# First norm's affine rows and the layer projection's rows asked for one at a time, at pairs 0, 1 and 3 of the output projection's second half

## The chip, the cores and the metric

The kernel runs on one core of a Trainium2 chip. The metric is the device time of one execution in microseconds. Before the change the median of three runs is 1655.25 us (1653.83 to 1656.07).

## The reference, cut to what matters

One decoder layer over 256 tokens of width 2048, all in float32. The change lies where step 2 below ends (the output projection and the first LayerNorm) and where step 4's second factor is prepared.

```
# 1. two token mixers (gated linear attention, forgetting attention) -> merged (256 x 2048)
x = layer_norm(ALPHA * x + merged @ w_out, ln1_g, ln1_b)          # 2.
g = causal_dwconv(x @ w_gate, conv_w, conv_b)                     # 3.
x = layer_norm(ALPHA * x + (gelu(g) * (x @ w_up)) @ w_down, ln2_g, ln2_b)
x = x + sigmoid(x @ w_ple_gate) * (p @ w_ple_proj)                # 4.

layer_norm(x, g, b) = (x - mean) * rsqrt(var + 1e-5) * g + b      # along the 2048 channels
```

The products keep float32 accuracy: each float32 operand is split into a high part (rounded to the matmul's format, "hi") and a rest ("lo"), and hi*hi, hi*lo and lo*hi are summed in PSUM.

## The kernel before, in words

**Weights.** The weights lie in memory as numbered units of 128 x 2048 floats (1 MB), and are used in the order of their numbers. A unit comes in two halves of 512 KB (`raw130_0`, `raw130_1`). For each half, `prep` (lines 191 to 230) issues a load on SP's queue into one of four "raw" buffers (line 205); then ScalarE (ACT) copies it to a "hi" buffer (line 212), and VectorE (DVE) subtracts hi from raw into a "lo" buffer (line 217); then TensorE (PE) multiplies. So the load of a half waits until DVE has made the lo of the half four places before it in the raw ring. `unit` (line 235) prepares up to two units ahead of the one that it hands out. There are six hi and six lo buffers.

**SP's queue** is kept in the order in which the Python code asks for the loads (line 118). The instructions of the other engines are put in order by the compiler's scheduler, which also follows priorities (`tc.high_priority`, `tc.keep_in_program_order`); each engine then works strictly in that order.

**The output projection** is `residual("wo", ...)` (line 1232; the function is at line 1053). It has two column halves, `nh` 0 and 1, of eight units each: 120 to 127, then 128 to 135. One unit covers a pair of 128-row blocks of the contraction, so the code counts "pairs" 0 to 7 in each half. A normal pair has 24 matmuls of 512 columns (line 334): two blocks, two token halves, three products, two banks. In the first half pairs 1, 2, 4 and 5 go another way with seven products (line 354). In the second half the last two pairs (units 134, 135) are held back as a tail (`tail=2`) and done token half by token half, so that the LayerNorm of the first 128 tokens (`t` = 0) can begin while the second 128 are still being multiplied.

**Loads between the pairs.** `mid` maps a pair to calls made after that pair: in the first half `mid1` loads the residual `z1` at pairs 2 and 3, and `mid1g` at pair 7 loads the norm's gain and bias, each a row of 2048 floats broadcast to 128 partitions (`lnb00` and `lnb01`, 1 MB of SBUF each, `load_gain`, line 1109). In the second half `mid1x` at pair 0 only reserves the four buffers of `x1T` (the norm's transposed output), and `ple_prep(0)` at pair 3 (line 1115) loads the layer projection's first half (`praw00`, `praw01`, 512 KB each, in raw buffers) and the transposed `p` (`pTr`, 256 KB), with the same hi and lo split on ACT and DVE. All of these but `praw` and `pTr` sit in a pool of 15 buffers of 8 KB per partition (`s8`).

**The first LayerNorm** (`ln_steps`, line 1001, run from `end1`, line 1149): the evacuation adds PSUM to `z1` (line 1066) and takes statistics (1067); DVE joins them (1009, 1010), GpSimd raises to the power -1/2 (1011), DVE makes the shift (1012). Column groups 1 and 3 are normalised on ACT (line 1025), and get gain and bias only after the transposition, as per-partition scalars (1043 on ACT, 1045 on DVE, taking turns within one group). Groups 0 and 2 get gain and bias from `lnb00` and `lnb01` on DVE (1020, 1022). The order of the groups is 1, 0, 3, 2. Each group is transposed on PE (line 1033) into one of two PSUM buffers, so the third transposition waits until the first group has been read, the fourth until the second has. Between them PE works on the layer projection (`pp`, line 334). Then the MLP's first units (136, 137, 138) begin on the first 128 tokens (line 303), and the normalised rows are later multiplied by gain and bias (line 1104) and written out for the next residual.

Of the kernel before, what the change touches and what calls it, by code (L numbers as in the profile page):

```python
# [19 lines left out]
P = 128  # L20
# [28 lines left out]
WOW = ((1, 2, 4, 5), ())  # L49
# [15 lines left out]
def tile_block(ctx: ExitStack, tc: tile.TileContext, wu, xw, wfv, wpp, xT_in, x_in, pT_in, wlr,  # L65
               chan, gnorm, lng, ident_in, mask_in, cmask_in, out):
    nc = tc.nc
# [15 lines left out]
    st1 = [cst.tile([P, 4, 6], F32, name=f"st1{t}") for t in range(2)]  # L83
# [3 lines left out]
    def s8(shape, dt=F32, name=None):  # L87
        t = big.tile([P, S8W], dt, tag="S8", name=name)
        n = int(np.prod(shape[1:]))
        t = t[:shape[0], :n]  # L90
        if len(shape) == 3:
            return t.rearrange("p (a b) -> p a b", b=shape[2])
        if len(shape) == 4:
            return t.rearrange("p (a b c) -> p a b c", b=shape[2], c=shape[3])
        return t
# [10 lines left out]
    def t2(name):  # L106
        return sm.tile([P, 512], F32, tag="t2", bufs=6, name=name)
# [7 lines left out]
    def copy(o, i, scale=1.0):  # L115
        nc.scalar.activation(o, i, AF.Copy, bias=0.0, scale=scale)
# [796 lines left out]
    mT = [s8([P, 4, 512], F32R, name=f"mT{i}") for i in range(4)]  # L913
# [139 lines left out]
    def residual(name, act, K, zs, stats, mid, done=None, end=None, ws=((), ())):  # L1053

        for nh in range(2):
            def zp(t, c, nh=nh):
                g = 2 * nh + c
                return zs[t][:, g * 512:g * 512 + 512]

            def ev(t, c, ps, nh=nh, zp=zp):  # L1060
                zc = zp(t, c)
                with tc.high_priority(P_STAT):
                    if ws[nh]:
                        nc.vector.tensor_tensor(zc, zc, ps, ALU.add)
                    else:
                        nc.vector.scalar_tensor_tensor(zc, zc, ALPHA, ps, ALU.mult, ALU.add)
                    nc.vector.bn_stats(stats[t][:, 2 * nh + c, :], zc)

            def joined(ms, zp=zp):
                p1, p5, p7, p6 = ms  # L1070
                u = t2("ju")

                def onto(t, c, p):
                    with tc.high_priority(P_STAT):
                        nc.vector.scalar_tensor_tensor(zp(t, c), zp(t, c), ALPHA, p, ALU.mult,
                                                       ALU.add)

                def plus(o, a, p):
                    with tc.high_priority(P_STAT):
                        nc.vector.tensor_tensor(o, a, p, ALU.add)  # L1080

                with tc.high_priority(P_STAT):
                    tc.keep_in_program_order(nc.scalar.activation(u, p1, AF.Copy, bias=0.0,
                                                                  scale=1.0))
                    tc.keep_in_program_order(nc.vector.scalar_tensor_tensor(
                        zp(0, 0), zp(0, 0), ALPHA, p1, ALU.mult, ALU.add))
                plus(u, u, p6)
                onto(0, 1, u)
                plus(u, u, p7)
                onto(1, 0, u)  # L1090
                plus(u, u, p5)
                onto(1, 1, u)
                plus(zp(0, 1), zp(0, 1), p5)

            x_half(f"{name}{nh}", act, K, ev, tail=2 if nh == 1 else 0, mid=mid[nh],
                   done=done if nh == 1 else None, end=end if nh == 1 else None, ws=ws[nh],
                   joined=joined, lean=name == "dn")

    def affine(zs, gb_, after, gs=range(4)):
        for t in range(2):  # L1100
            for g in gs:
                zc = zs[t][:, g * 512:g * 512 + 512]
                for b, op in zip(gb_, (ALU.mult, ALU.add)):
                    tc.keep_in_program_order(nc.vector.tensor_tensor(
                        zc, zc, b[:, g * 512:g * 512 + 512], op))
                    yield
            after(t)

    def load_gain(li):
        gb_ = [s8([P, 2048], name=f"lnb{li}{i}") for i in range(2)]  # L1110
        for i in range(2):
            nc.sync.dma_start(gb_[i], lng[2 * li + i].broadcast_to([P, 2048]))
        return gb_

    def ple_prep(half):

        w = [s8([P, 2048], F32R, name=f"pw{half}{i}") for i in range(2)]
        pt_ = s8([P, 2, 512], F32R, name=f"pTs{half}")
        pTs = [pt_[:, k, :] for k in range(2)]
        for k in range(2):  # L1120
            raw = ring.tile([P, 1024], F32, tag="raw", bufs=4, name=f"praw{half}{k}")
            nc.sync.dma_start(raw, wpp[half, :, k * 1024:k * 1024 + 1024])
            o = slice(k * 1024, k * 1024 + 1024)
            copy(w[0][:, o], raw)
            nc.vector.tensor_tensor(w[1][:, o], raw, w[0][:, o].bitcast(F32), ALU.subtract)
        pT = t2("pTr").rearrange("p (k t) -> p k t", t=S)
        nc.sync.dma_start(pT, pT_in)
        for k in range(2):
            copy(pTs[k][:, 0:256], pT[:, k, :])
            nc.vector.tensor_tensor(pTs[k][:, 256:512], pT[:, k, :],  # L1130
                                    pTs[k][:, 0:256].bitcast(F32), ALU.subtract)
        return w, pTs

    z1 = [s8([P, 2048], name=f"z1{t}") for t in range(2)]
    gain = [None, None]

    def mid1(t):
        nc.sync.dma_start(z1[t], x_in[t])

    def mid1g():  # L1140
        gain[0] = load_gain(0)

    x1T = []
    pq, first = [], []

    def mid1x():
        x1T.extend(s8([P, 4, 512], F32R, name=f"x1T{g}") for g in range(4))
# [81 lines left out]
                    turn1(G[3])  # L1229
            first.extend(ps)  # L1230

    residual("wo", mT, 16, z1, st1, ({2: lambda: mid1(0), 3: lambda: mid1(1), 7: mid1g}, {0: mid1x, 3: lambda: pq.append(ple_prep(0))}), end=end1, ws=WOW)
    mixers.append(affine(z1, gain[0], lambda t: nc.gpsimd.dma_start(x1d[t], z1[t]),
                         [g for g in range(4) if g not in AFF_DVE]))

# [92 lines left out]
    def mid2a():  # L1328
        gain[1] = load_gain(1)
# [5 lines left out]
    pb, pq = [], []  # L1335
# [224 lines left out]
```

## Time and profile before

| | |
|---|---|
| median of three runs | 1655.25 us |
| the profiled execution's own time | 1654.46 us |
| its span, first to last instruction | 1652.7 us |
| PE busy in the span | 1645.3 us |
| DVE, ACT busy | 1235.4, 882.4 us |
| moved by DMA | 394.23 MB, 239 GB/s in the mean |
| granted PE clock | 1.0 |

In the rows of the profile, times are in microseconds from the span's start. A timeline row reads: start, length, engine, line, operation, what it writes and reads, the count of merged instructions, and in brackets how long the engine sat idle before it and what ended that. PE's matmuls are pipelined: their lengths overlap, and one follows another by less than its length. SPq rows are DMA issues; where ACT waits for a load, its row begins just after the load has landed.

### The profile page before, as it was taken

How to read it: one execution, taken by the hardware profiler on the slowest of the kernel's cores; microseconds unless marked ns; L12 is line 12 of the kernel's file. 1: busy time of each engine (PE TensorE's matmuls, PEld its weight loads, DVE VectorE, ACT ScalarE, POOL GpSimd, SP SyncE). 2: the span in 40 equal slices, each digit the busy share in tenths (PEclk: the TensorE clock that was granted, in tenths of full speed). 3: DMA queues.
4: the chain of work that ended last, by engine and by line, in shares of the span. 5: the costliest groups of instructions: out<-in, count | busy, mean ns of one | idle time of the engine just before them, and what ended most of it. 6: DMA issues, size and time to landing. Idle time of an engine off the chain costs nothing.

```text
span 1652.7 us, 24308 instructions
## 1 busy us (share of the span) xinstructions
PE 1645.3 (100%) x8956; PEld 1427.4 (86%) x8956; DVE 1235.4 (75%) x1819; ACT 882.4 (53%) x1268; POOL 94.7 (6%) x217
## 2 busy tenths in 40 slices
PE   9999999999999999999999999999999999999998
PEld 8988888888888888888888888888888888888887
DVE  6656658768756767787688788888887687888884
ACT  6745445545555555555465545554455565466643
POOL 0000000000000100000010011111110011010000
PEclk9999999999999999999999999999999999999999
DMA  7665555555553875567747678888886588799354
GB/s 298 234 203 178 165 188 181 180 180 176 182 180 128 322 278 199 194 207 292 270 169 235 229 253 325 330 319 333 327 288 228 196 296 304 285 335 355 144 188 169
DMA packets 107527, 394.23 MB, mean 239 GB/s; under 512 B 12504, under 2 KB 13408, under 8 KB 104464
## 3 DMA queue, kind: packets, MB, share of 16 engines
q1 hardware_dynamic: 97296, 354.72, 61.9%
q0 software_dynamic: 9968, 37.76, 6.0%
q8 instruction: 70, 1.15, 0.3%
q14 instruction: 49, 0.40, 0.1%
q10 hardware_dynamic: 144, 0.20, 0.0%
HBM read 365.36 MB, written 27.27 MB: 238 GB/s over the span
## 4 chain that ended last, share of the span: by engine, by line
PE 94%; DMA 3%; DVE 2%; ACT 1%; issue 0%; SPq 0%; POOL 0%; ACTq 0%; DVEq 0%
PE psu L290 9%; PE psg L290 9%; PE psm L290 7%; PE dn L334 7%; PE gr L334 5%; PE gv L334 5%; PE pg L334 5%; PE psu L292 5%; PE psg L292 5%; PE psm L292 4%; PE psa L290 4%; PE fv L496 3%; DMA raw<-in_wu_dram 2%; PE dn L354 2%; PE dn0m L354 2%; PE psfq L290 2%
## 5 line engine op out<-in xcount | busy, mean ns | idle before, releaser
L217 DVE TENSOR_TENSOR lo<-raw,hi 128x1024 fp32r<-128x1024 f32 x502 | 611.4, 1224 | 257.8 <-ACT hi L212 255.8
L212 ACT ACTIVATE hi<-raw 128x1024 fp32r<-128x1024 f32 x502 | 528.9, 1059 | 464.8 <-DMA raw<-in_wu_dram 127.5
L290 PE MATMUL psu<-x1T,hi 128*128 128x512 f32 x688 | 236.0, 389 | 0.0
L290 PE MATMUL psg<-x1T,hi 128*128 128x512 f32 x672 | 230.5, 389 | 0.0
L292 PE MATMUL psu<-x1T,lo 128*128 128x256 f32 x688 | 189.9, 276 | 0.0
L292 PE MATMUL psg<-x1T,lo 128*128 128x256 f32 x672 | 185.5, 276 | 0.0
L290 PE MATMUL psm<-xT,hi 128*128 128x512 f32 x512 | 175.8, 391 | 0.0
L290 PEld LDWEIGHTS psu<-x1T,hi 128*128 128x128 f32 x688 | 129.2, 188 | 26.6
L290 PEld LDWEIGHTS psg<-x1T,hi 128*128 128x128 f32 x672 | 126.1, 188 | 26.1
L292 PE MATMUL psm<-xT,lo 128*128 128x256 f32 x512 | 141.4, 276 | 0.0
L292 PEld LDWEIGHTS psu<-x1T,lo 128*128 128x128 f32 x688 | 129.2, 188 | 0.0
L292 PEld LDWEIGHTS psg<-x1T,lo 128*128 128x128 f32 x672 | 126.1, 188 | 0.0
L290 PEld LDWEIGHTS psm<-xT,hi 128*128 128x128 f32 x512 | 96.1, 188 | 19.8
L334 PE MATMUL dn<-hi,hT 128*128 128x512 f32 x352 | 97.8, 389 | 0.0
L292 PEld LDWEIGHTS psm<-xT,lo 128*128 128x128 f32 x512 | 96.2, 188 | 0.2
L290 PE MATMUL psa<-oT,hi 128*128 128x512 f32 x256 | 87.8, 389 | 0.0
L334 PEld LDWEIGHTS dn<-hi,hT 128*128 128x128 f32 x352 | 66.0, 188 | 13.7
L334 PE MATMUL gv<-hi,xT 128*128 128x512 f32 x256 | 72.3, 394 | 0.0
L334 PE MATMUL gr<-hi,xT 128*128 128x512 f32 x256 | 72.1, 394 | 0.0
L292 PE MATMUL psa<-oT,lo 128*128 128x256 f32 x256 | 70.7, 276 | 0.0
L334 PE MATMUL pg<-hi,x2T 128*128 128x512 f32 (+1 forms) x224 | 60.0, 376 | 0.0
L290 PEld LDWEIGHTS psa<-oT,hi 128*128 128x128 f32 x256 | 48.1, 188 | 10.0
(356 smaller groups left out, 3075.6 us busy)
## 6 DMA issues: line engine op xcount, KB each, us to landing
raw<-in_wu_dram SPq DMA_DIRECT2D x528, 512.0 KB, 4.8
comb<-in_wu_dram SPq DMA_DIRECT2D x22, 768.0 KB, 8.7
tsd<-comb POOLq DMA_DIRECT2D x22, 512.0 KB, 7.2
top<-tsd SPq DMA_DIRECT2D x22, 512.0 KB, 6.1
fvraw<-in_wfv_dram SPq DMA_DIRECT2D x15, 524.0 KB, 7.9
rawf<-in_wu_dram SPq DMA_DIRECT2D x14, 512.0 KB, 9.4
top<-in_wu_dram SPq DMA_DIRECT2D x22, 256.0 KB, 7.0
hi<-hsd POOLq DMA_DIRECT2D x22, 256.0 KB, 5.2
```

Of the source, the lines that this page charges most:

```text
L212: c = nc.scalar.activation(hi, raw, AF.Copy, bias=0.0, scale=1.0)
L217: return nc.vector.tensor_tensor(lo, raw, hi.bitcast(F32), ALU.subtract)
L290: nc.tensor.matmul(ps, lhsT=hi[i // 8 if hoff == 0 else 0][:, w0 % 1024:w0 % 1024 + P], rhs=a[:, kt % 4, :], start=first and i == 0, stop= ...
L292: nc.tensor.matmul(ps[:, 256:512], lhsT=lo[i // 8 if hoff == 0 else 0][:, w0 % 1024:w0 % 1024 + P], rhs=a[:, kt % 4, 0:256], start=False, ...
L334: nc.tensor.matmul(bs[j][:, 0:m], lhsT=x, rhs=v[:, o:o + m], start=first and i == 0, stop=last and i == 2)
L354: nc.tensor.matmul(ps, lhsT=a, rhs=v, start=m and first and i == 0, stop=m and last and i == 2)
L496: nc.tensor.matmul(fbk[t][c][:, 0:n], lhsT=x, rhs=w[:, o:o + n], start=kt == 0 and i == 0, stop=kt == 15 and i == 2)
```

## The change

The output projection's second half gets other calls between its pairs. `ple_prep(0)` moves from pair 3 to pair 0; the gain row is asked for at pair 1 and the bias row at pair 3, instead of both at pair 7 of the first half; `x1T`'s buffers are reserved at pair 3 instead of 0. `load_gain`, which the second norm uses too, issues the same two loads as before.

```
-    def load_gain(li):
-        gb_ = [s8([P, 2048], name=f"lnb{li}{i}") for i in range(2)]
-        for i in range(2):
-            nc.sync.dma_start(gb_[i], lng[2 * li + i].broadcast_to([P, 2048]))
+    def load_row(li, i):
+        row = s8([P, 2048], name=f"lnb{li}{i}")
+        nc.sync.dma_start(row, lng[2 * li + i].broadcast_to([P, 2048]))
+        return row
+    def load_gain(li):
+        gb_ = []
+        for i in range(2):
+            gb_.append(load_row(li, i))
         return gb_
...
-    def mid1g():
-        gain[0] = load_gain(0)
+    gain1 = gain[0] = []
+    def mid1g(i):
+        gain1.append(load_row(0, i))
...
-    residual("wo", mT, 16, z1, st1, ({2: lambda: mid1(0), 3: lambda: mid1(1), 7: mid1g}, {0: mid1x, 3: lambda: pq.append(ple_prep(0))}), end=end1, ws=WOW)
+    residual("wo", mT, 16, z1, st1, ({2: lambda: mid1(0), 3: lambda: mid1(1)}, {0: lambda: pq.append(ple_prep(0)), 1: lambda: mid1g(0), 3: lambda: (mid1x(), mid1g(1))}), end=end1, ws=WOW)
```

**SP, the loads from unit 131 on.** SP's queue before, from the bias row to the layer projection's loads:

```order
L1112 DMA lnb01_7570<-in_lng_dram 128x2048
L205 DMA raw130_0_7585<-in_wu_dram 128x1024
L205 DMA raw130_1_7591<-in_wu_dram 128x1024
L205 DMA raw131_0_7625<-in_wu_dram 128x1024
L205 DMA raw131_1_7631<-in_wu_dram 128x1024
L205 DMA raw132_0_7661<-in_wu_dram 128x1024
L205 DMA raw132_1_7667<-in_wu_dram 128x1024
L205 DMA raw133_0_7697<-in_wu_dram 128x1024
L205 DMA raw133_1_7703<-in_wu_dram 128x1024
L1122 DMA praw00_7736<-in_wpp_dram 128x1024
L1122 DMA praw01_7740<-in_wpp_dram 128x1024
L1127 DMA pTr_7744<-in_pT_dram 128x512
```

And now, from the place behind unit 130 to unit 134:

```order
L1127 DMA praw00_7620<-in_wpp_dram 128x1024
L1127 DMA praw01_7624<-in_wpp_dram 128x1024
L1132 DMA pTr_7628<-in_pT_dram 128x512
L205 DMA raw131_0_7634<-in_wu_dram 128x1024
L205 DMA raw131_1_7640<-in_wu_dram 128x1024
L1111 DMA lnb00_7670<-in_lng_dram 128x2048
L205 DMA raw132_0_7672<-in_wu_dram 128x1024
L205 DMA raw132_1_7678<-in_wu_dram 128x1024
L205 DMA raw133_0_7708<-in_wu_dram 128x1024
L205 DMA raw133_1_7714<-in_wu_dram 128x1024
L1111 DMA lnb01_7748<-in_lng_dram 128x2048
L205 DMA raw134_0_7750<-in_wu_dram 128x1024
```

The layer projection's two halves take the raw buffers in which unit 131 lay before, and every half from 131 to 133 comes two places later in the ring; from 134 on the places are the old ones. The two 1 MB rows have moved from ahead of 130 to ahead of 132 and of 134. On ACT and DVE the projection's splits have moved with their loads, from between 133 and 134 to between 130 and 131.

**DVE in the first LayerNorm.** DVE before, from the first group's bias (line 1022) to the shift of the second token half (line 1012 of `mv_7879`); `z10` is the first token half, `z11` the second, `lny_7920` the affine step of group 1:

```order
L1022 SCALAR_TENSOR_TENSOR z10_7247<-z10_7247,mv_7878,lnb01_7570 128x512
L1066 SCALAR_TENSOR_TENSOR z11_7248<-z11_7248,wo1_10_7583 128x512
L1020 SCALAR_TENSOR_TENSOR z10_7247<-z10_7247,mv_7878,lnb00_7569 128x512
L1067 BN_STATS st11_85<-z11_7248 128x6
L1022 SCALAR_TENSOR_TENSOR z10_7247<-z10_7247,mv_7878,lnb01_7570 128x512
L1066 SCALAR_TENSOR_TENSOR z11_7248<-z11_7248,wo1_11_7584 128x512
L1045 TENSOR_SCALAR lny_7920<-ptl101_7915,chn_81 128x128
L1067 BN_STATS st11_85<-z11_7248 128x6
L1009 BN_AGGR mv_7879<-st11_85 128x2
L1010 TENSOR_SCALAR mv_7879<-mv_7879 128x1
L1045 TENSOR_SCALAR lny_7920<-ptl101_7915,chn_81 128x128
L1012 TENSOR_SCALAR mv_7879<-mv_7879 128x1
```

And now the same twelve:

```order
L1066 SCALAR_TENSOR_TENSOR z11_7248<-z11_7248,wo1_10_7579 128x512
L1022 SCALAR_TENSOR_TENSOR z10_7247<-z10_7247,mv_7878,lnb01_7748 128x512
L1067 BN_STATS st11_85<-z11_7248 128x6
L1020 SCALAR_TENSOR_TENSOR z10_7247<-z10_7247,mv_7878,lnb00_7670 128x512
L1066 SCALAR_TENSOR_TENSOR z11_7248<-z11_7248,wo1_11_7580 128x512
L1022 SCALAR_TENSOR_TENSOR z10_7247<-z10_7247,mv_7878,lnb01_7748 128x512
L1067 BN_STATS st11_85<-z11_7248 128x6
L1045 TENSOR_SCALAR lny_7920<-ptl101_7915,chn_81 128x128
L1009 BN_AGGR mv_7879<-st11_85 128x2
L1010 TENSOR_SCALAR mv_7879<-mv_7879 128x1
L1012 TENSOR_SCALAR mv_7879<-mv_7879 128x1
L1045 TENSOR_SCALAR lny_7920<-ptl101_7915,chn_81 128x128
```

The evacuations of the second token half stand one place earlier, and the second of group 1's affine steps now stands behind line 1012, which waits for GpSimd, instead of ahead of it.

**ACT in the same place.** ACT before, with the weight copies of units 137 and 138 and the affine steps of group 1:

```order
L212 ACTIVATE hi137_1_7841<-raw137_1_7839 128x1024
L1043 ACTIVATE lny_7920<-ptl101_7915,chn_81 128x128
L212 ACTIVATE hi138_0_8003<-raw138_0_8001 128x1024
L1043 ACTIVATE lny_7920<-ptl101_7915,chn_81 128x128
L212 ACTIVATE hi138_1_8008<-raw138_1_8006 128x1024
L116 ACTIVATE x1T1_7622<-lny_7920 128x4x128
```

And now:

```order
L212 ACTIVATE hi137_1_7841<-raw137_1_7839 128x1024
L1043 ACTIVATE lny_7920<-ptl101_7915,chn_81 128x128
L212 ACTIVATE hi138_0_8003<-raw138_0_8001 128x1024
L212 ACTIVATE hi138_1_8008<-raw138_1_8006 128x1024
L1043 ACTIVATE lny_7920<-ptl101_7915,chn_81 128x128
L116 ACTIVATE x1T1_7745<-lny_7920 128x4x128
```

The second affine step of group 1 now stands behind both copies of unit 138. A further exchange, of the same two kinds of DVE instruction, lies just ahead: the first evacuation (line 1066 on `wo1_00`) now stands before `lo136_1` instead of behind it.

## The prediction

> **What bounds the kernel now.** I read the page first, then the table of windows, PE's waits and timeline, and last the timelines of SP, ACT and DVE from 780 to 845 us, where all that moves lies. The page says that the chain that ended last is PE:
>
> ```profile
> span 1652.7 us, 24308 instructions
> PE 94%; DMA 3%; DVE 2%; ACT 1%; issue 0%; SPq 0%; POOL 0%; ACTq 0%; DVEq 0%
> ```
>
> So moving loads pays only if PE waits for something that they hold up. The table of windows (PE's busy time stands first, DMA share and GB/s last) shows the second half of the output projection and the LayerNorm behind it:
>
> ```profile
> core 0: us, PE busy (x) PEld busy (x) DVE busy (x) ACT busy (x) POOL busy (x), PEclk, DMA share, GB/s
> 797.00:812.00 15.00, 15.00 (x67) 12.11 (x66) 10.35 (x9) 5.82 (x6) 0.00 (x0) 1.00 0.70 234
> 836.00:845.00 9.00, 7.89 (x43) 6.12 (x42) 6.91 (x16) 7.67 (x13) 0.55 (x1) 1.00 0.00 0
> ```
>
> PE is full while the projection runs and loses 1.11 us in the norm. PE's timeline shows where, and when it needs units 131 and 132 (each lo is used behind two matmuls on hi):
>
> ```profile
> 780.56 1.07 PE L334 MATMUL wo<-hi,mT 128*128 128x512 f32 x4
> ...
> 808.49 0.62 PE L334 MATMUL wo<-lo,mT 128*128 128x512 f32 x2
> ...
> 813.93 0.62 PE L334 MATMUL wo<-lo,mT 128*128 128x512 f32 x2
> ...
> 826.17 0.61 PE L334 MATMUL wo<-hi,mT 128*128 128x512 f32 x2
> 826.81 0.50 PE L334 MATMUL wo<-lo,mT 128*128 128x512 f32 x1
> ...
> 840.57 0.66 PE L1033 MATMUL ptl<-ident,z 128*128 128x128 f32 x4 [0.93 <-DVE lny L1045]
> ...
> 842.80 0.66 PE L1033 MATMUL ptl<-ident,z 128*128 128x128 f32 x4 [0.18 <-DVE x1T L855]
> ```
>
> Two matmuls take 0.62 us where one takes 0.39, so one follows another by 0.23. Counting 24 to a unit on from 780.56, where unit 126 begins behind the last pair of the seven-product kind, the row at 808.49 is the first lo of unit 131 and that at 813.93 of 132. The row at 826.81 is the first use of `lo135_1`; it should have come at 826.17 + 0.45 = 826.62, so PE lost 0.19 there. The third transposition waited 0.93 us for DVE, the fourth 0.18.
>
> **The feed of units 131 to 134.** The issues on SP, then the copies to hi on ACT, which begin about 0.1 us after a load has landed:
>
> ```profile
> 781.85 1.00 SPq L1112 DMA_DIRECT2D lnb<-in_lng_dram  x2
> 797.86 0.33 SPq L205 DMA_DIRECT2D raw<-in_wu_dram  x1
> 799.00 0.33 SPq L205 DMA_DIRECT2D raw<-in_wu_dram  x1
> 800.13 0.33 SPq L205 DMA_DIRECT2D raw<-in_wu_dram  x1
> 804.20 0.33 SPq L205 DMA_DIRECT2D raw<-in_wu_dram  x1
> 812.05 0.33 SPq L205 DMA_DIRECT2D raw<-in_wu_dram  x1
> ```
>
> ```profile
> 788.03 1.06 ACT L212 ACTIVATE hi<-raw 128x1024 fp32r<-128x1024 f32 x1 [0.19 <-DMA raw<-in_wu_dram]
> 794.18 1.06 ACT L212 ACTIVATE hi<-raw 128x1024 fp32r<-128x1024 f32 x1 [5.08 <-DMA raw<-in_wu_dram]
> 795.41 1.06 ACT L212 ACTIVATE hi<-raw 128x1024 fp32r<-128x1024 f32 x1 [0.18 <-DMA raw<-in_wu_dram]
> 801.86 1.06 ACT L212 ACTIVATE hi<-raw 128x1024 fp32r<-128x1024 f32 x1 [5.38 <-DMA raw<-in_wu_dram]
> 804.68 1.06 ACT L212 ACTIVATE hi<-raw 128x1024 fp32r<-128x1024 f32 x1 [1.76 <-DMA raw<-in_wu_dram]
> 807.17 1.06 ACT L212 ACTIVATE hi<-raw 128x1024 fp32r<-128x1024 f32 x1 [1.43 <-DMA raw<-in_wu_dram]
> 818.84 1.06 ACT L212 ACTIVATE hi<-raw 128x1024 fp32r<-128x1024 f32 x1 [0.94 <-DMA raw<-in_wu_dram]
> ```
>
> And DVE, where the lo are made:
>
> ```profile
> 796.63 4.61 DVE L217 TENSOR_TENSOR lo<-raw,hi 128x1024 fp32r<-128x1024 f32 x4
> 819.93 2.48 DVE L217 TENSOR_TENSOR lo<-raw,hi 128x1024 fp32r<-128x1024 f32 x2 [0.71 <-ACT hi L212]
> 827.95 2.46 DVE L217 TENSOR_TENSOR lo<-raw,hi 128x1024 fp32r<-128x1024 f32 x2 [1.19 <-ACT hi L212]
> 831.64 0.67 DVE L1066 SCALAR_TENSOR_TENSOR z<-z,wo 128x512 f32<-128x512 f32 x1
> ```
>
> The four lo from 796.63 are those of 129 and 130: DVE makes them late, behind the first half's evacuation, and in the same order after the change. Each frees a raw buffer, and SP's issues at 797.86, 799.00 and 800.13 follow them. Before, the first three were `raw131_0`, `raw131_1` and `raw132_0`; they had landed when ACT began at 801.86, 804.68 and 807.17. Now the first two are `praw00` and `praw01`, `pTr` follows at once, and `raw131_0` is third.
>
> What is removed is little: the two 1 MB rows went out at 781.85 and delayed unit 130 (5.08 us of idle ACT ahead of 794.18), but its lo waited for DVE until after 796.63 anyway. So that delay cost nothing, and its removal brings nothing.
>
> What is added. When does `raw131_0` land? The upper bound is the same place in the old burst, 807.1, plus `pTr` in front of it. A full queue delivers 512 KB in 1.23 us (795.41 - 794.18; between 788.03 and 794.18 come two rows and half a unit, five times 512 KB, in 6.15), so `pTr`, half of that, makes it 807.7. The lower bound is the lone load's 801.76 (3.9 us after its issue) and from there that full rate: 1.23 + 0.62 + 1.23 more, 804.8. I take 807.0, nearer to the burst with the same issue times. Then hi is done at 807.1 + 1.06 = 808.2, lo at 809.4. PE wants it at 808.49: a new wait of 0.9 us.
>
> From there, at 1.23 us per 512 KB: `raw131_1` 808.2, `lnb00` 810.7, `raw132_0` (issued at 804.20 at the earliest, behind the row) 811.9; its lo is done at 814.3. PE wants it at 813.93 + 0.9: no second wait, with half a microsecond left. `raw134_0` takes that buffer now, so it is issued at 814.3 instead of 812.05, and has `raw132_1`, 133 and the bias row ahead of it: 813.1, 814.4, 815.6, 818.1, so it lands at 819.3 and its lo begins at 820.5. Before it began at 819.93: **0.6 us later**. `raw136_0` takes its place in the ring, so the pair of lo that began at 827.95 begins 0.6 later too.
>
> Which of these two delays reaches the end? DVE ran from 827.95 without a break to the second evacuation at 831.64. By the count, PE had finished that bank at 826.81 + 14 x 0.23 + 0.39 = 830.4, so DVE was 1.2 us behind PE there, and DVE sets the time of the norm. A delay of PE by 0.9 less the 0.19 that no longer arises stays inside that, and inside the 0.93 that PE idles later. **So the new wait is paid out of idle time that was there; the 0.6 us on DVE is not.** The exchange of the first evacuation with `lo136_1` leaves the sum of DVE's work up to the statistics the same: 0.
>
> **The order inside the LayerNorm.** DVE and ACT before:
>
> ```profile
> 838.70 0.41 DVE L1045 TENSOR_SCALAR lny<-ptl,chn 128x128 f32<-128x128 f32 x1
> ...
> 840.11 0.40 DVE L1045 TENSOR_SCALAR lny<-ptl,chn 128x128 f32<-128x128 f32 x1
> 840.86 0.21 DVE L1012 TENSOR_SCALAR mv<-mv 128x1 f32<-128x1 f32 x1 [0.35 <-POOL mv L1011]
> ...
> 842.07 0.68 DVE L855 TENSOR_TENSOR x1T<-ptl,x1T 128x512 fp32r<-128x512 f32 x1
> ```
>
> ```profile
> 838.57 1.05 ACT L212 ACTIVATE hi<-raw 128x1024 fp32r<-128x1024 f32 x1
> 839.52 0.44 ACT L1043 ACTIVATE lny<-ptl,chn 128x128 f32<-128x128 f32 x1
> ```
>
> The third transposition waited for the second affine step of DVE, done at 840.51. That step now stands behind line 1012, which waits for GpSimd until 840.86; an instruction follows it by some 0.13, so the step runs from 840.99 to 841.39. On ACT the affine step ahead of it now stands behind another copy of 0.95 (839.52 - 838.57): 840.47 to 840.91, which agrees. So the third transposition comes 0.88 later, at 841.45. From there PE has 842.80 - 840.57 - 0.18 = 2.05 of work to the fourth: 843.5 instead of 842.8, and the operand that it waited 0.18 for (842.07 + 0.68, likewise some 0.6 later) is there. **0.7 us**, with 0 (if the work before it shortens as much) and 0.9 as bounds. Queued behind line 1012 on DVE is all of `x1T`, so the units of the MLP begin that much later; nothing behind shows idle PE that could give it back. Elsewhere the change permutes buffers of the pool one for one, with equal lifetimes: 0. The gain row lands at 810.7, the bias row at 818.1, and both are first read after 833: 0.
>
> Sum: 0.6 + 0.7 = +1.3 us. Against the profiled execution (1654.46, of which the span is 1652.7) this gives 1655.8; against the median of 1655.25, 0.8 above that execution, 1656.5.
>
> **A page against the trace.** A lone 512 KB took 801.76 - 797.86 = 3.9 us here. The Trainium skill, "DMA: Bandwidth & Descriptors", section "Anatomy of one DMA", puts a DMA at 2.0 us plus its bytes at 436 GB/s (fitted for GpSimd's path), as an estimate 3.2 us for these 512 KB, and a burst at 1.2 us for each. By it `raw131_0` would land near 804 and PE would not wait at all; the row at 807.17 (9.3 us after the burst began, for three such loads) says otherwise, and the trace decides.
>
> **The rivals.** (a) *The queue runs full at once.* At 1.23 us per 512 KB behind 801.76, `raw131_0` lands at 804.8, `raw132_0` at 809.7, its lo is done at 812.1, `raw134_0` is issued as before and lands 5.0 us later at 817.1, and DVE's chain comes 1.6 earlier, as far as PE allows. With the 0.7 of the norm's order: -0.9; with that at nothing, no more than the 1.11 + 0.19 that PE idles: -1.3. For it speaks the rate behind 788.03, against it the burst behind 797.86. 1654.0 to 1655.2. It is also what the page above would make of the burst. (b) *The queue stays slow, and the kernel is slower.* The window from 797 to 812 ran at 234 GB/s, 2.24 us per 512 KB. At that pace `raw131_0` lands at 807.4, `raw132_0`, behind the 1 MB row, at 816.3, its lo is done at 818.7, 4.4 later than in the sum, and `raw134_0` with it: 0.6 + 4.4 + 0.7 = +5.7, 1661.0. It decides from the point where `lo132_0` comes after 816.3, 2 us later than I have it. Against it: up to five transfers are then in flight, as behind 788.03, not three. (c) *It does nothing*, since all is hidden: 1655.2. For it: PE idle and DVE behind PE, so both terms are small; against it: the new order on DVE is certain.
>
> **How the numbers follow.** The forecast, with its neighbours from 0 to +3.3, gets 0.58, (a) and (c) together 0.24, (b) 0.14, and 0.04 stays for what I don't see. The bound for "same" is 0.2%, 3.3 us, about what a measurement of this kernel can tell from no change. Faster than that needs more than the idle that there is: the 0.04. Slower is (b), from +3.3 on: 0.14. Same: 0.58 + 0.24 = 0.82. The range goes from -1.4 (a) to +3.9, between the forecast and (b), and leaves out most of (b) and the unseen: 1653.8 to 1659.2.
>
> **What would show it.** Right: PE's first lo of unit 131 waits 0.5 to 1.7 us for DVE or DMA, the wait of 0.19 at 135 is gone, the third transposition waits longer than 0.93 for line 1045, and the MLP begins 1 to 2 us later. Wrong: no wait at 131 (then (a)); a wait at 132 of microseconds (then (b)); the norm's waits as before; or a shift that arises elsewhere, after 870 or before 797.

## The result and the profile after

| | before | after |
|---|---|---|
| median of 22 runs each, taken side by side | 1654.86 us | 1657.58 us |
| ratio, 95% interval | | 1.0019 (1.0013 to 1.0025) |
| span of the profiled execution | 1652.7 us | 1655.4 us |

The change makes the kernel 0.19% slower: by the ratio +3.1 us (2.2 to 4.1), where +1.3 was forecast. It lies inside the range, but is over twice the forecast.

PE's waits after, with their places, from PE's timeline; from 780 to 870 us it shows no others. The first row is the first matmul of unit 126, which stands at 780.56 before. The profiled execution of after reaches it 0.78 earlier, and nothing that the change touches comes ahead of it; so all times below that are compared between two kernels are counted from this matmul in each (its row stands first in each PE block).

```profile
779.78 1.07 PE L334 MATMUL wo<-hi,mT 128*128 128x512 f32 x4
...
808.43 0.73 PE L334 MATMUL wo<-hi,mT 128*128 128x512 f32 x2 [1.06 <-ACT hi L212]
809.69 0.73 PE L334 MATMUL wo<-lo,mT 128*128 128x512 f32 x2 [0.53 <-DVE lo L217]
...
837.50 0.66 PE L1033 MATMUL ptl<-ident,z 128*128 128x128 f32 x4 [0.78 <-ACT z L1025]
...
839.39 0.60 PE L1033 MATMUL ptl<-ident,z 128*128 128x128 f32 x4
...
843.14 0.66 PE L1033 MATMUL ptl<-ident,z 128*128 128x128 f32 x4 [1.76 <-DVE lny L1045]
...
847.00 2.12 PE L303 MATMUL psg<-x1T,hi 128*128 128x256 f32 x16
```

PE waits 1.06 + 0.53 = 1.59 us at unit 131 and nowhere else in the projection. The first transposition now waits for ACT's normalised rows (0.78), the third 1.76 for line 1045. The MLP starts at 847.00 - 779.78 = 67.22, against 844.67 - 780.56 = 64.11 before: 3.11 later, and nothing behind it gives that back: the span ends 1655.4 - 779.78 = 875.6 behind unit 126, against 1652.7 - 780.56 = 872.1. The second transposition and the first matmul of the MLP before:

```profile
837.65 0.60 PE L1033 MATMUL ptl<-ident,z 128*128 128x128 f32 x4
...
844.67 2.13 PE L303 MATMUL psg<-x1T,hi 128*128 128x256 f32 x16
```

The feed, on ACT after (hi of 131_0, 132_0, 132_1, 133_0, 133_1, 134_0, 136_0 and 136_1), and SP's issues of 132 and 133, of the bias row and of `raw134_0`:

```profile
807.33 1.06 ACT L212 ACTIVATE hi<-raw 128x1024 fp32r<-128x1024 f32 x1 [1.04 <-DVE pTs L1135]
...
812.27 1.06 ACT L212 ACTIVATE hi<-raw 128x1024 fp32r<-128x1024 f32 x1 [2.65 <-PE wo L334]
813.51 1.06 ACT L212 ACTIVATE hi<-raw 128x1024 fp32r<-128x1024 f32 x1 [0.18 <-DMA raw<-in_wu_dram]
815.40 1.06 ACT L212 ACTIVATE hi<-raw 128x1024 fp32r<-128x1024 f32 x1 [0.83 <-DMA raw<-in_wu_dram]
817.66 1.06 ACT L212 ACTIVATE hi<-raw 128x1024 fp32r<-128x1024 f32 x1 [1.19 <-DMA raw<-in_wu_dram]
821.39 1.06 ACT L212 ACTIVATE hi<-raw 128x1024 fp32r<-128x1024 f32 x1 [2.67 <-DMA raw<-in_wu_dram]
...
828.02 1.06 ACT L212 ACTIVATE hi<-raw 128x1024 fp32r<-128x1024 f32 x1 [1.87 <-DMA raw<-in_wu_dram]
830.55 1.06 ACT L212 ACTIVATE hi<-raw 128x1024 fp32r<-128x1024 f32 x1 [1.47 <-DMA raw<-in_wu_dram]
```

```profile
803.45 7.79 SPq L205 DMA_DIRECT2D raw<-in_wu_dram  x4
811.29 0.42 SPq L1111 DMA_DIRECT2D lnb<-in_lng_dram  x1
814.62 0.33 SPq L205 DMA_DIRECT2D raw<-in_wu_dram  x1
```

And what DVE makes of it, from the lo of 134 and 135 to the statistics:

```profile
822.49 4.92 DVE L217 TENSOR_TENSOR lo<-raw,hi 128x1024 fp32r<-128x1024 f32 x4 [2.51 <-ACT hi L212]
829.12 1.23 DVE L217 TENSOR_TENSOR lo<-raw,hi 128x1024 fp32r<-128x1024 f32 x1 [1.71 <-ACT hi L212]
830.26 0.68 DVE L1066 SCALAR_TENSOR_TENSOR z<-z,wo 128x512 f32<-128x512 f32 x1
831.64 1.23 DVE L217 TENSOR_TENSOR lo<-raw,hi 128x1024 fp32r<-128x1024 f32 x1 [0.70 <-ACT hi L212]
...
834.82 0.26 DVE L1009 BATCH_NORM_AGGREGATE mv<-st 128x2 f32<-128x24 f32 x1
```

The lo of 134 begin at 822.49 - 779.78 = 42.71, against 819.93 - 780.56 = 39.37 before: 3.34 later, not 0.6. The second lo of 136 (831.64) waits 0.70 for its hi, and the statistics begin at 55.04. Before, line 1009 stood here:

```profile
833.08 0.26 DVE L1009 BATCH_NORM_AGGREGATE mv<-st 128x2 f32<-128x24 f32 x1
```

That is 52.52: the norm begins 2.52 later.

### The profile page after: what moved, and what is told of

It reads as the page before. It is cut to its first block, busy times and chain, and to the rows that moved or that the text cites. A ratio compares the mean times of both kernels' runs of the same rounds, so it can differ in the third digit from the quotient of the medians.

```text
span 1655.4 us, 24309 instructions
## 1 busy us (share of the span) xinstructions
PE 1645.9 (99%) x8956; PEld 1427.0 (86%) x8956; DVE 1234.1 (75%) x1819; ACT 882.1 (53%) x1268; POOL 92.2 (6%) x217
## 4 chain that ended last, share of the span: by engine, by line
PE 98%; DVE 1%; ACT 0%; DMA 0%; issue 0%; DVEq 0%; ACTq 0%
PE psu L290 9%; PE psg L290 9%; PE dn L334 7%; PE psm L290 7%; PE gr L334 5%; PE gv L334 5%; PE pg L334 5%; PE psu L292 5%; PE psg L292 5%; PE psm L292 4%; PE psa L290 4%; PE fv L496 3%; PE wo L334 3%; PE dn L354 3%; PE dn0m L354 2%; PE psq L290 2%
```

## The experiments

Theories: **D**, the loss passes through DVE: the loads of unit 134 come late, with them the lo of 136, and these stand ahead of the statistics; the norm's new order adds 0.85. **P**: PE's own wait at unit 131 passes through. **S**: the scheduler's new order alone. Within D, **D1**: the two rows make 134 late; **D2**: the projection's loads do, by taking two places in the ring. All runs were timed in five rounds beside the kernel before (11 runs each). In microseconds; the three columns in the middle are counted from the first matmul of unit 126 in each profile:

| kernel | hi of 134 begins | statistics begin | MLP begins | against before, 95% interval |
|---|---|---|---|---|
| before | 38.28 | 52.52 | 64.11 | |
| after | 41.61 | 55.04 | 67.22 | +3.1 (2.2 to 4.1) |
| projection's loads alone | 38.77 | 53.71 | 65.32 | +0.2 (-1.3 to +1.7) |
| these, and one row ahead of 132 | 39.82 | 53.95 | 65.55 | +1.8 (+0.3 to +3.1) |
| rows alone | 41.95 | 55.94 | 68.14 | +3.6 (+2.2 to +5.0) |

**PE 1.6 us late and nothing else** (kernel before):

```
-                mm(i, unit(), (0, 1))
+                w = unit()
+                mm(i, w, (0, 1))
+                if name == "wo1" and i == 2:
+                    ah = act[1][:, 1, 0:P]
+                    for _ in range(7):
+                        nc.tensor.matmul(banks[0][0][0], lhsT=ah, rhs=w[0][1][:, 0:512],
+                                         start=False, stop=False)
```

> The kernel before, with seven products of unit 130 issued a second time behind that unit, so that PE comes to unit 131 7 x 0.23 = 1.6 us later and no load, copy or order is touched (the products are counted twice in the output). Theory D (the loss passes through DVE: unit 134's loads come late, with them both lo of 136, and these stand ahead of the statistics): PE's delay lies mostly inside the idle time of the norm, +0.3 us against before (0 to +0.6), and the third transposition waits less than 0.93. Theory P (PE's wait of 1.6 us at unit 131 simply passes through to the end): +1.4 to +1.6. Theory S (the scheduler's new order on DVE and ACT is the cost, the loads are harmless): 0.

Measured: 1.0005 (0.9996 to 1.0014), +0.8 us, between the theories and telling neither apart. The trace:

```profile
781.09 1.07 PE L334 MATMUL wo<-hi,mT 128*128 128x512 f32 x4
...
837.32 0.65 PE L1039 MATMUL ptl<-ident,z 128*128 128x128 f32 x4
...
842.12 0.66 PE L1039 MATMUL ptl<-ident,z 128*128 128x128 f32 x4 [0.92 <-DVE lny L1051]
...
846.24 2.11 PE L303 MATMUL psg<-x1T,hi 128*128 128x256 f32 x16
```

```profile
829.52 2.44 DVE L217 TENSOR_TENSOR lo<-raw,hi 128x1024 fp32r<-128x1024 f32 x2 [2.72 <-ACT hi L212]
```

The MLP begins at 65.15, 1.04 late, and the third transposition waits as long as ever. But DVE was late too: it began the lo of 136 at 829.52 - 781.09 = 48.43, against 47.39 before, though no load had been touched. So this run can't say what PE's wait costs when DVE is punctual. That it is absorbed is not shown.

**After's loads, before's order in the norm** (three order pins, no other edit):

```
-                with tc.high_priority(P_STAT):
+                with tc.high_priority(P_STAT), (tc.issue_after(held[136, 1])
+                                                if (name, nh, t, c) == ("wo", 1, 0, 0) else ExitStack()):
                     if ws[nh]:
                         nc.vector.tensor_tensor(zc, zc, ps, ALU.add)
...
+                with tc.issue_after(held["DVE"]) if nm == "l1" and t == 1 else ExitStack():
                     nc.vector.tensor_scalar(mv[:, 4:5], mv[:, 0:1], -1.0, mv[:, 3:4], ALU.mult, ALU.mult)
...
+            with tc.issue_after(held["ACT"]) if (u, h) == (138, 1) else ExitStack():
                 c = nc.scalar.activation(hi, raw, AF.Copy, bias=0.0, scale=1.0)
```

Here `held` keeps the second lo of 136 and, of the first group's affine steps, the second on DVE (line 1045) and the second on ACT (1043).

> The kernel after with all its loads, but the order of before put back on DVE and ACT in the norm: both lo of 136 ahead of the first evacuation, the second affine step ahead of line 1012, the second line 1043 ahead of the second copy of 138. Theory D: raw136_1 lands as late as after, so the statistics begin even 0.7 later than after (the evacuation now stands behind the late lo), and the norm's order gives back 0.85: +2.4 to +3.2 us against before, about as after. Theory P: after's wait without the order's 0.85, +1.4. Theory S: 0, at most +0.5.

Measured: 1.0022 (1.0013 to 1.0031), +3.6 us (2.2 to 5.1), where D had 2.4 to 3.2. Theory S falls: with the old order the loss is all there. DVE and PE of this run:

```profile
780.65 1.07 PE L336 MATMUL wo<-hi,mT 128*128 128x512 f32 x4
...
839.30 0.65 PE L1036 MATMUL ptl<-ident,z 128*128 128x128 f32 x4 [1.79 <-ACT z L1028]
...
841.18 0.60 PE L1036 MATMUL ptl<-ident,z 128*128 128x128 f32 x4
...
844.08 0.66 PE L1036 MATMUL ptl<-ident,z 128*128 128x128 f32 x4 [0.91 <-DVE lny L1048]
```

```profile
832.97 1.22 DVE L219 TENSOR_TENSOR lo<-raw,hi 128x1024 fp32r<-128x1024 f32 x1 [1.77 <-ACT hi L214]
...
836.62 0.26 DVE L1011 BATCH_NORM_AGGREGATE mv<-st 128x2 f32<-128x24 f32 x1
```

DVE stands still for 1.77 us before the second lo of 136, the statistics begin at 836.62 - 780.65 = 55.97, later than after, and the first transposition waits 1.79 for what they lead to. From the beginning of that lo to the statistics it takes 836.62 - 832.97 = 3.65 here (3.90 before), and 834.82 - 831.64 = 3.18 after. So the exchange of the first evacuation with that lo, in the change, is a gain of 0.5 to 0.7: the evacuation fills the time in which the lo waits. The second to the third transposition takes 844.08 - 841.18 = 2.90, as before (840.57 - 837.65 = 2.92, 837.65 being the second's start there) and not as after (3.75): the norm's order is worth its 0.85. The two all but cancel.

**Both lo of 136 behind the first two normalised groups**, in after and in before:

```
-            elif u in LATE_LO:
+            elif u in LATE_LO or u == 136:
...
+            with tc.issue_after(held["norm"]):      # second line 1022 of the first token half
+                for lo in later[136]:
+                    lo()
```

> The kernel after with all its loads, but both lo of 136 made behind the first two normalised groups on DVE instead of ahead of the statistics (they are needed only where the MLP begins). Theory D: the statistics no longer wait for raw136; what is left is PE's own wait of 1.6 at unit 131, which now sets the norm's time: about +0.5 us against before (-0.3 to +1.0), and some 1.4 above the same edit made to the kernel before. Theory P: as after, +2.7. Theory S: equal to the same edit made to the kernel before.

> The same edit as in the run before this one, made to the kernel before: both lo of 136 behind the first two normalised groups. Theory D: DVE was 1.2 us behind PE at the second evacuation, so the statistics begin up to 1.1 us earlier, and PE idles less in the norm: -0.6 us (-1.1 to 0). Theories P and S: 0, since nothing else moves; if the lo of 136 then come too late for the MLP's first unit, slower by up to 1.

Measured: 1.0020 (1.0011 to 1.0029), +3.3 us, for after; 1.0004 (0.9996 to 1.0013), +0.7, for before. The times miss both forecasts of D; by its time alone the first would fit theory P (+2.7). The first half of the mechanism holds: in after the statistics (line 1010 here) come at 832.95 - 780.61 = 52.34 instead of 55.04, and no transposition waits for ACT or for the affine step. The second half does not; PE of the run on after:

```profile
780.61 1.07 PE L335 MATMUL wo<-hi,mT 128*128 128x512 f32 x4
...
844.99 1.10 PE L304 MATMUL psg<-x1T,hi 128*128 128x256 f32 x8
847.26 1.35 PE L304 MATMUL psg<-x1T,hi 128*128 128x256 f32 x8 [1.17 <-DVE x1T L1049]
```

```profile
831.50 0.69 DVE L1067 SCALAR_TENSOR_TENSOR z<-z,wo 128x512 f32<-128x512 f32 x1 [1.30 <-PE wo L335]
...
832.95 0.26 DVE L1010 BATCH_NORM_AGGREGATE mv<-st 128x2 f32<-128x24 f32 x1
```

```profile
844.90 1.06 ACT L213 ACTIVATE hi<-raw 128x1024 fp32r<-128x1024 f32 x1 [1.03 <-DMA raw<-in_wu_dram]
845.87 0.61 ACT L116 ACTIVATE x1T<-lny 128x512 fp32r<-128x512 f32 x1
```

The lo of 136 frees the raw buffer of 138. Made late, it makes that load late, and ACT, in order, waits for it with the copies of `x1T` queued behind; so PE stands still for 1.17 in the middle of the MLP's first unit. Of the 2.7 us gained at the statistics this profile keeps 1.4 at its end (1654.8 - 780.61 = 874.2, against 1655.4 - 779.78 = 875.6 after), and the times, +3.3 with 1.5 either way, show none.

The pair also shows what PE's own wait does when the lo of 136 are out of the way. In both runs DVE now waits for PE at the second evacuation (1.30 in the row above, 1.33 in the run on before), so PE sets the statistics. PE comes to its last matmul of the projection 1.4 later in the run on after (836.51 - 780.61 = 55.90, against 834.77 - 780.31 = 54.46), and its delay is still there at the statistics (52.34 against 831.20 - 780.31 = 50.89) and at the MLP (844.99 - 780.61 = 64.38 against 843.27 - 780.31 = 62.96): the 1.4 between the two that D had forecast. The times differ by more, 2.6; what makes up the rest no run shows.

**The projection's loads alone; with one row; the rows alone.** The `mid` maps of the three kernels:

```
first half {..., 7: lambda: (mid1g(0), mid1g(1))}, second {0: lambda: (mid1x(), pq.append(ple_prep(0)))}
first half {..., 7: lambda: mid1g(0)},             second {0: lambda: pq.append(ple_prep(0)), 1: lambda: mid1g(1), 3: mid1x}
first half {...},                                  second {0: mid1x, 1: lambda: mid1g(0), 3: lambda: (mid1g(1), pq.append(ple_prep(0)))}
```

> Only the layer projection's loads are moved (pair 0); both 1 MB rows stay at pair 7 of the first half, and the order on DVE and ACT in the norm is that of before. Counted from the start of unit 126 on PE, raw134_0 lands at 38.2 us before and at 41.5 after, the statistics (line 1009) begin at 52.5 and 55.0. Theory D1 (raw134 is late because the two rows stand ahead of 132 and 134): PE still waits 1.6 at unit 131, but raw134_0 lands at 38.4 (37.7 to 39.2) and the statistics begin by 53.2; the time is +0.3 to +1.2, what is left of PE's wait. Theory D2 (it is late because the projection's loads take unit 131's buffers and every load shifts in the ring): raw134_0 beyond 40.5, +2.5. Theory P (PE's wait passes through whole): +1.5.

> The projection's loads at pair 0 as after, the gain row back at pair 7 of the first half, the bias row at pair 1: so one row stands ahead of 132 as after, and none ahead of 134; order on DVE and ACT as before. Theory D1: lo of 132 comes as late as after and raw134_0 is issued as late, but with no row in front of it lands 5.5 us after its issue: 40.3 (39.5 to 41.0) from the start of unit 126, the statistics begin 1.5 to 2.5 later than before, +2.0 us (+1.0 to +3.0). Theory D2: as the run with the projection alone. Theory P: +1.5.

> Only the two rows are moved (pairs 1 and 3); the projection's loads stay at pair 3 and x1T's reservation at pair 0; the order on DVE and ACT in the norm comes out as after. No wait at unit 131. Theory D1: raw134_0, behind both rows and the projection's loads, lands 39.2 to 40.2 from the start of unit 126, the statistics begin about 1 to 1.5 later, and the norm's order adds 0.85: +2.0 us (+1.0 to +2.8). Theory D2: the order alone, +0.85. Theory P: 0, at most +0.85.

Measured: 1.0001 (0.9992 to 1.0010), +0.2; 1.0011 (1.0002 to 1.0019), +1.8; 1.0022 (1.0013 to 1.0030), +3.6. The first, with the projection's loads alone, on PE and on ACT:

```profile
779.96 1.07 PE L334 MATMUL wo<-hi,mT 128*128 128x512 f32 x4
...
808.33 0.74 PE L334 MATMUL wo<-hi,mT 128*128 128x512 f32 x2 [0.78 <-ACT hi L212]
809.59 0.73 PE L334 MATMUL wo<-lo,mT 128*128 128x512 f32 x2 [0.52 <-DVE lo L217]
```

```profile
818.73 1.06 ACT L212 ACTIVATE hi<-raw 128x1024 fp32r<-128x1024 f32 x1 [1.37 <-DMA raw<-in_wu_dram]
```

PE's wait at 131 is there (0.78 + 0.52 = 1.30), and the time is that of before, within 1.7. The hi of 134 begins at 818.73 - 779.96 = 38.77, half a microsecond late, which is within what profiles with the same loads differ by (last section); the statistics, at 53.71, are later than the 53.2 that I had as their limit. With one row ahead of 132, the hi of 134 is at 820.27 (unit 126 at 780.45 in that run), 1.5 late, and the statistics are 1.43 late, just short of the 1.5 to 2.5 forecast; the time is as forecast:

```profile
820.27 1.06 ACT L212 ACTIVATE hi<-raw 128x1024 fp32r<-128x1024 f32 x1 [2.35 <-DMA raw<-in_wu_dram]
```

The rows alone, with no load of the projection ahead of 131, on ACT, DVE and PE:

```profile
822.42 1.06 ACT L212 ACTIVATE hi<-raw 128x1024 fp32r<-128x1024 f32 x1 [1.16 <-DMA raw<-in_wu_dram]
```

```profile
836.41 0.26 DVE L1009 BATCH_NORM_AGGREGATE mv<-st 128x2 f32<-128x24 f32 x1
```

```profile
780.47 1.07 PE L334 MATMUL wo<-hi,mT 128*128 128x512 f32 x4
...
839.10 0.66 PE L1033 MATMUL ptl<-ident,z 128*128 128x128 f32 x4 [1.27 <-ACT z L1025]
...
844.74 0.66 PE L1033 MATMUL ptl<-ident,z 128*128 128x128 f32 x4 [1.77 <-DVE lny L1045]
```

That is 41.95 and 55.94, as late as after or later, and the loss is the whole one. I had expected 2.0 (1.0 to 2.8) for it; the late 134 was under-sized there once more. PE does not wait at unit 131 in this run; it waits 0.18 + 0.25 + 0.25 + 0.72 = 1.40 for the lo of 134 and 135, which are late with their loads. So the loss needs no wait at 131, and theory P, which had at most 0.85 here, falls as the whole account. D1 stands and D2 falls: **the two 1 MB rows are the cause, the projection's move costs nothing that the times show.** A small cost of it is not excluded: the interval reaches to +1.7, and in its profile the MLP begins 1.2 later. By the loads, against the run with the projection's loads alone, the row ahead of 132 makes 134 come 1.05 later (39.82 - 38.77), and the row ahead of 134 another 1.8 (41.61 - 39.82); the times, +0.2, +1.8 and +3.1, rise with them, though their intervals overlap.

**A faster version from what was learnt?** Two more tries on the kernel before: both lo of 136 late and the copies of 138 pinned behind those of `x1T`; then only the second lo of 136 late, with 138's second copy pinned.

```
+            if u == 138:                            # second try: (u, h) == (138, 1)
+                es.enter_context(tc.issue_after(held["x1T"]))
+                es.enter_context(tc.high_priority(P_STAT))
             c = nc.scalar.activation(hi, raw, AF.Copy, bias=0.0, scale=1.0)
...
+            elif u in LATE_LO or (u, h) == (136, 1):   # second try
```

> The kernel before with both lo of 136 behind the first two normalised groups, as in an earlier run, and now both copies of 138 on ACT behind the copies of x1T, so that they no longer hold these up (that cost the earlier run 1.45 us of idle PE in the MLP's first unit). Theory D: the statistics begin 1.9 us earlier, the MLP's first unit 1.15 earlier and without a stop: -1.1 us (-1.5 to -0.3), a version faster than both. Rival: unit 138's copies now come too late for the third unit of the MLP, or hold up the second token half's norm: 0 to +1.

> The kernel before with only the second lo of 136 taken from ahead of the statistics to behind the second token half's shift (line 1012), and the second copy of 138 on ACT behind the copies of x1T. The first lo stays, so unit 138's first load keeps its time. Theory D: the statistics begin 1.2 us earlier (PE's second bank is full at 830.4 and DVE is no longer behind it), the third transposition's wait of 0.93 all but goes, and x1T then waits 0.85 for the moved lo: -0.4 us (-1.1 to +0.2). Rival: ACT's moved copy of 138 holds up the norm of the second token half, as in the run before this: 0 to +1.5.

Measured: 1.0016 (1.0007 to 1.0024), +2.6, and 1.0006 (0.9997 to 1.0015), +1.0. Theory D, with -1.1 and -0.4, misses both; the second fits its rival, the first lies beyond its rival's +1. PE in the second:

```profile
780.25 1.07 PE L339 MATMUL wo<-hi,mT 128*128 128x512 f32 x4
...
843.37 2.12 PE L308 MATMUL psg<-x1T,hi 128*128 128x256 f32 x16
845.75 0.66 PE L1039 MATMUL ptl<-ident,z 128*128 128x128 f32 x4 [0.26 <-ACT z L1031]
...
851.85 0.39 PE L308 MATMUL psg<-x1T,hi 128*128 128x256 f32 x1 [0.79 <-DVE x1T L1055]
```

The MLP begins at 63.12, 1.0 before its time, as D has it, and the second token half gives it back: 0.26 for ACT's norm and 0.79 for DVE's `x1T`. In the first try PE stands still for 2.2 us at that place. What these edits gain ahead of the MLP is asked back within it, and none of these versions beats the kernel before.

## Why the prediction was half right

- *A new wait at unit 131, 0.9 us (0 to 1.7).* Came, at 1.59. `raw131_0` landed 807.33 - 779.78 + 780.56 - 0.1 = 808.0 in before's time, not at 807.0, and past the upper bound of 807.7: the burst was a little slower than the one that set the bound.
- *It is paid out of idle time.* In the kernel after it adds nothing, but only because DVE is later still: the first transposition waits another 0.78 for it. By itself a wait of this size is not paid so in the profiles: with the lo of 136 out of the way, PE's delay of 1.4 comes through to the MLP whole. With the projection's loads alone and with the padded PE, the MLP begins 1.2 and 1.0 later, while DVE is late as well. What it is worth in time stays open: +0.2 and +0.8, with 1.5 either way.
- *DVE's chain is what sets the time of the norm.* Right for the kernel after: moving 136's lo away brings the statistics back to their time, and putting the order back takes nothing off the loss. That the time itself comes back with the statistics is not shown: the run that moved the lo away lost it again in the MLP.
- *The term of +0.6: mis-sized.* This is the step that failed: "From there, at 1.23 us per 512 KB". The loads to 132_1 did come at that pace, about 1.0 late with `raw131_0` (hi of 132_0 at 812.27 + 0.78 = 813.05, where the sum has the load at 811.9); but `raw133_0` and `raw133_1` came 815.40 - 813.51 = 1.9 and 817.66 - 815.40 = 2.3 apart. Behind them the pace held again: the bias row and `raw134_0` took 821.39 - 817.66 = 3.73, three times 1.24. So the bias row and `raw134_0` came 1.0 + 1.7 = 2.7 later than in the sum: 3.3 at the lo of 134, instead of 0.6. Counted from its issue, `raw134_0` landed 821.39 - 0.1 - 814.62 = 6.7 us later, just as before (818.84 - 0.1 - 812.05 = 6.7), where the sum left it 5.0; the other 1.1 is the issue itself, at 814.62 + 0.78 = 815.4 in before's time instead of 814.3. Why the loads of 133 were slow no run shows. Their issue alone does not say it: both, and the bias row, were issued by 811.3, before `raw132_1` had landed at 813.4, and yet only 221 GB/s came in from 813 to 815 us, against 420 from 807 to 809.
- *136 follows 134.* Right, and only the second half counts: `raw136_0` came back soon, `raw136_1` 2.5 later (830.55 - 828.02), so that its lo is 831.64 - 779.78 = 51.86 against 827.95 + 1.23 - 780.56 = 48.62 before, 3.24 late.
- *The exchange of the first evacuation with `lo136_1`: 0.* It was priced as if DVE never waited there. With the lo late it saves 3.90 - 3.18 = 0.72.
- *The norm's order: 0.88 at the third transposition, 0.7 at the fourth.* Right: 3.75 - 2.92 = 0.83 at the third, and of it 3.11 - 2.52 = 0.6 when the MLP begins.
- *The sum.* 3.24 - 0.72 + 0.59 = 3.11 when the MLP begins (the last term is what is left of it), against 0.6 + 0.7 = 1.3. Of the four signs of being right three came; the MLP began 3.1 later and not 1 to 2. That the time still lies inside the range is luck as far as the mechanism goes: the upper end, +3.9, was set by rival (b), not by the spread of these terms.
- *The rivals.* Of (b), a queue that stays slow with `lo132_0` beyond 816.3, the place was right and the pace wrong: that lo is done when `raw134_0` is issued, 814.62 + 0.78 = 815.4 in before's time, short of the point from which it decides, and PE never waited at 132. Of the delay that it saw coming through 132, most came through 133 instead. (a) and (c) are out by the interval.

The estimate from the Trainium skill's "DMA: Bandwidth & Descriptors", section "Anatomy of one DMA", in the prediction had `raw131_0` near 804 and no wait; the run has 808.0 and a wait of 1.59. The Trainium skill's sum for one DMA gave neither the landing nor the wait of these loads, of which several overlap.

## What to carry to other kernels

A load in a ring of buffers lands at its issue plus its time in flight, and its issue waits for the last use of a buffer some places back: follow a delay through that recurrence, with times in flight from the rows, and not with the queue's best pace throughout. Before moving a large load "to where it is needed", look at what it will stand ahead of: at its old place these rows delayed a unit whose consumer was busy anyway; at the new one they delayed units whose second operand stood, in program order, ahead of a serial chain. And an edit that makes one consumer later makes the next load into its buffer later too: what it gains at one place is asked back one turn of the ring on.

## What the runs showed of the hardware

- The same load behind the same loads does not take the same time. Up to unit 135 five profiles have before's loads in before's order (before, the padded kernel and three that only move lo or copies of 136 and 138), and there the hi of 134 begins 37.3 to 39.0 us behind the start of unit 126; in the three with after's loads it is 41.0 to 41.8. In the padded kernel DVE began the lo of 134 at 821.21 - 781.09 = 40.12, against 39.37 before, with every load and order as before:

```profile
821.21 2.47 DVE L217 TENSOR_TENSOR lo<-raw,hi 128x1024 fp32r<-128x1024 f32 x2 [1.11 <-ACT hi L212]
```

  So a microsecond or more of a chain of loads, read from one profile, can be chance: the projection's loads alone (38.77) lie inside the spread, one row ahead of 132 (39.82) is 0.8 beyond it, and after and the rows alone stand clear.
- Of two loads that are issued 1.1 us apart into an empty queue, the second came 2.1 to 3.8 us behind the first in the eleven profiles, not 1.23: 804.68 - 801.86 = 2.82 before.
